# A hybrid decoder layer on one core: its first row tile staged, and the gating, the bank saves and the mix loads of its gated-linear-attention stage put elsewhere

## The chip, the core and the metric

The kernel runs on one core of a Trainium2 chip. TensorE (PE in the rows, PEld for its weight loads) multiplies and transposes into PSUM banks; VectorE (DVE) and ScalarE (ACT) empty the banks; GpSimd (POOL) and SyncE (SP) issue DMAs. Each engine works through its own instructions in order and waits where an operand, a bank or a buffer is not ready. The metric is device microseconds (us) of one execution.

## What is computed

```python
hn = rms_norm(h, norm_mix)
gq, gk, gv, gr, ga, sq, sk, sv = split(hn @ w_in)           # T=1024 rows, D=1024
o_gla = gla_mixer(gq, gk, gv, gr, ga, ...)                  # 4 heads, d_k=64, d_v=128, chunks of 64
o_swa = swa_mixer(sq, sk, sv, rel_bias, sinks)              # window 128
h = h + concat([o_gla, o_swa]) @ w_out
h = h + cross_attn(rms_norm(h, norm_cross), rms_norm(mem, norm_mem), w_q, w_k, w_v, w_o)
h = h + conv_ffn(rms_norm(h, norm_ffn), w_up, conv_w, conv_b, w_down)
return rms_norm(h, norm_final)

# the part of gla_mixer behind the recurrence
o = o * rsqrt(mean(o * o, -1) + EPS) * gla_gain             # per head
return o.reshape(T, 512) * silu(gr)
```

## The kernel before

All data are float32. A product is made of three TensorE passes over operands split into a high and a low part: `split` (L105) has ACT cast the high part (L109, with a gain L112) and DVE subtract it to get the low part (L110, with a gain L113), and `mm3` (L138) multiplies high by high (L140), high by low (L141) and low by high (L142). PSUM has eight banks in this part of the kernel: two with the role F, four S, two O; a tile of a role takes the bank whose last tile has been emptied. Weights pass through three staging buffers (`st`) and six slots (`w`, three pairs), so a load can start only when the split of the load three before it is done.

**The start (`rows_a`, L449).** The 1024 rows of x come in eight row tiles of 128 rows (`load_x`, tiles `gr` and `prob`, 512 KB each); the weights for 272 columns of w_in come in three staged portions, for k = 0 to 2, 3 to 5 and 6 to 7 (`row_weights`, L423). The weights are loaded first, then the row tiles. For each row tile PE transposes eight 128x128 blocks into two S banks (L404), ACT and DVE split them into `xh` and `xl`, ACT sums the squares (`sumsq`, L188), and PE makes 8 x 3 products of 272 columns (`row_tile`). PE's order is written out: it transposes row tiles 0 and 1, then makes the products of tile 0, transposes tile 2, makes the products of tile 1, and so on. DVE multiplies each staged portion by the gain `norm_mix` (L124) ahead of its split. The other engines' order is left to a scheduler.

**The GLA stage (`gla`, L650).** The chunk recurrence runs over four pairs of row tiles (i = 0, 2, 4, 6). For a pair PE makes the state sums (L709) and the attention blocks (L739, two S banks), the outputs (`gla_products`, L758 and L765, two F banks); ACT squares them (L775), DVE sums (L776), both find the reciprocal root, and ACT scales the outputs into `o` (L787, eight instructions). One pair later `gla_output` (L790) transposes `o` into two S banks (L799), DVE gates each bank with `gla_gain` and `gr` (L802, tiles `eb`), and the result is split into `x` tiles (`og`). The orders of PE, DVE and ACT are the program's order here.

Between these steps `more(count)` (L658) runs portions of another job, the cross-attention keys and values of the 256 memory rows. `multiply(n)` makes the products of portion n; `prepare(n + 3)` loads and splits the weights of portion n + 3. Portions 0 to 7 are the values: four of them fill two O banks of 512 columns, which `save` (L346) empties in four pieces of 256 columns (`la`, ACT cast and DVE subtraction in turn, then a store by POOL's queue). Portions 8 to 15 are the keys, one O bank of 256 columns each. The calls are two portions ahead of each pair's products, two more behind the output of the third pair, three behind that of the fourth and four at the end of the loop.

**Behind it.** `swa_mix` (L907) loads the window attention's result from DRAM (`x<-ow_d`, eight loads of 512 KB on SP's queue). `mix_out` (L918) multiplies it and `og` by w_out (loads `st<-in_w_out_dram`, three DMAs a portion), then adds the residual `res`, which SP's queue loads from `xt_d`.

## Time and profile before

| | |
|---|---|
| median of 3 runs | 1338.66 us (1335.7 to 1339.94) |
| profiled execution | 1338.4 us, its span 1336.3 us |
| PE busy in the span | 1306.5 us (98%) |
| DVE, ACT, POOL busy | 920.8, 586.8, 86.4 us |

The profile is one execution; its times run from the start of its span, and 2.1 us of its time lie outside the span. In rows of the timeline the first number is the start, the second the duration, and the square bracket says how long the engine had stood idle before and what ended that.

### The profile page before, as it was taken

The page shows a single profiled execution, that of the slowest core. Times are in us where ns is not written, and L with a number is a line of the kernel's source. Part 1 is how long each engine was busy: PE and PEld are TensorE (multiplying, and loading weights), DVE is VectorE, ACT ScalarE, POOL GpSimd, SP SyncE. Part 2 cuts the span into 40 slices and gives each one's busy share as a digit, 9 for nine tenths or more (in the row PEclk, how much of TensorE's full clock was granted, in tenths as well). Part 3 has the DMA queues.
Part 4 walks back from the last instruction along what each step waited for, and adds up shares of the span by engine and source line. Part 5 has one row for each costly group of instructions (what it writes and reads, how often), then busy time and mean ns, then how long its engine had stood idle before and what let it go on. Part 6 is the DMA issues. An engine that isn't in the chain of part 4 may idle for free.

```text
span 1336.3 us, 17266 instructions
## 1 busy us (share of the span) xinstructions
PE 1306.5 (98%) x6575; PEld 1082.3 (81%) x6575; DVE 920.8 (69%) x1566; ACT 586.8 (44%) x1040; POOL 86.4 (6%) x150
## 2 busy tenths in 40 slices
PE   7999999999899999999999999999999999999997
PEld 6887777988788888888888888888888888788785
DVE  6848763367444344464469998888888887998766
ACT  5425545335333233453334554434443444454454
POOL 1400111101111000001100000000000000000000
PEclk9999999999999999999999999999999999999998
DMA  7642111144954422143321333222232138710203
GB/s 219 178 116 64 60 55 60 63 149 145 294 162 142 134 64 64 31 141 97 95 64 58 115 127 110 95 92 66 79 95 94 65 109 317 267 64 8 72 20 146
DMA packets 141528, 146.89 MB, mean 110 GB/s; under 512 B 15825, under 2 KB 108166, under 8 KB 141446
## 3 DMA queue, kind: packets, MB, share of 16 engines
q1 hardware_dynamic: 129974, 111.02, 27.1%
q0 software_dynamic: 10304, 32.68, 6.9%
q10 hardware_dynamic: 1168, 2.10, 0.4%
q8 instruction: 51, 0.84, 0.3%
q14 instruction: 31, 0.25, 0.1%
HBM read 109.06 MB, written 38.28 MB: 110 GB/s over the span
## 4 chain that ended last, share of the span: by engine, by line
PE 49%; issue 37%; DVE 6%; DMA 4%; POOL 2%; ACT 2%; SPq 1%; POOLq 0%; DVEq 0%; ACTq 0%
PE psF L140 9%; PE psF L142 9%; PE psF L141 9%; PE psF L1262 4%; PE psS L1262 3%; DVE w L110 2%; DMA st<-in_w_out_dram 2%; PE psT L1262 1%; PE psO L1262 1%; PE psO L140 1%; PE psO L141 1%; PE psO L142 1%; PE psO L897 1%; PE psS L844 1%; PE psS L884 1%
## 5 line engine op out<-in xcount | busy, mean ns | idle before, releaser
L109 ACT CAST w<-st 128x1024 fp32r<-128x1024 f32 (+2 forms) x165 | 145.2, 880 | 293.9 <-PE psF L141 106.4
L110 DVE TENSOR_TENSOR w<-st,w 128x1024 fp32r<-128x1024 f32 (+2 forms) x165 | 166.3, 1008 | 91.4 <-ACT w L109 90.4
L1184 DVE SCALAR_TENSOR_TENSOR uy<-uy,vec,uy 128x1023 f32<-128x1023 f32 (+1 forms) x88 | 112.0, 1278 | 0.9 <-ACT uy L1182 0.4
L1262 PE MATMUL psF<-w,w 128*128 128x512 f32 x330 | 92.9, 390 | 0.1
L1262 PE MATMUL psS<-w,w 128*128 128x512 f32 x330 | 92.4, 389 | 0.0
L1155 PE MATMUL psS<-a,w 128*128 128x512 f32 x360 | 86.5, 389 | 0.0
L140 PE MATMUL psF<-xh,w 128*128 128x512 f32 x208 | 82.9, 399 | 0.0
L141 PE MATMUL psF<-xl,w 128*128 128x512 f32 x208 | 81.4, 391 | 0.0
L142 PE MATMUL psF<-xh,w 128*128 128x512 f32 x208 | 81.4, 391 | 0.0
L1155 PEld LDWEIGHTS psS<-a,w 128*128 128x128 f32 x360 | 67.6, 188 | 14.0
L1155 PE MATMUL psF<-a,w 128*128 128x512 f32 x324 | 77.8, 389 | 0.0
L1262 PEld LDWEIGHTS psF<-w,w 128*128 128x128 f32 x330 | 61.8, 188 | 13.8 <-DVE w L110 0.8
L1262 PEld LDWEIGHTS psS<-w,w 128*128 128x128 f32 x330 | 62.0, 188 | 12.9
L1155 PEld LDWEIGHTS psF<-a,w 128*128 128x128 f32 x324 | 60.8, 188 | 12.6
L140 PE MATMUL psF<-act,w 128*128 128x512 f32 x176 | 69.4, 394 | 0.0
L141 PE MATMUL psF<-act,w 128*128 128x512 f32 x176 | 69.1, 392 | 0.0
L142 PE MATMUL psF<-act,w 128*128 128x512 f32 x176 | 68.7, 390 | 0.0
L1182 ACT ACTIVATE uy<-uy,vec 128x1024 f32<-128x1024 f32 x44 | 54.8, 1246 | 24.9 <-DVE uy L1175 17.2
L1155 PE MATMUL psS<-act,w 128*128 128x512 f32 x240 | 57.8, 389 | 0.0
L1155 PE MATMUL psS<-act,wx 128*128 128x512 f32 x240 | 57.6, 389 | 0.0
L1155 PEld LDWEIGHTS psS<-act,w 128*128 128x128 f32 x240 | 45.1, 188 | 9.4
L1155 PEld LDWEIGHTS psS<-act,wx 128*128 128x128 f32 x240 | 45.0, 188 | 9.3
(392 smaller groups left out, 3004.3 us busy)
## 6 DMA issues: line engine op xcount, KB each, us to landing
st<-in_w_up_dram SPq DMA_DIRECT2D x44, 512.0 KB, 3.9
g_d<-uy POOLq DMA_DIRECT2D x22, 512.0 KB, 2.9
act<-in_w_down_dram SPq DMA_DIRECT2D x12, 512.0 KB, 9.7
st<-g_d SPq DMA_DIRECT2D x10, 512.0 KB, 3.9
res<-g_d SPq DMA_DIRECT2D x10, 512.0 KB, 9.2
st<-in_w_in_dram SPq DMA_DIRECT2D x9, 512.0 KB, 6.2
xt_d<-pts POOLq DMA_DIRECT2D x16, 256.0 KB, 4.6
ow_d<-pts POOLq DMA_DIRECT2D x32, 128.0 KB, 3.2
```

Source lines behind the costliest of these rows:

```text
L109: h = nc.scalar.copy(out=hi, in_=src)
L110: l = nc.vector.tensor_tensor(out=lo, in0=src, in1=hi.bitcast(F32), op=ALU.subtract)
L140: mm(out, lhsT=lh, rhs=rh, start=start, stop=False)
L141: mm(out, lhsT=lh, rhs=rl, start=False, stop=False)
L142: mm(out, lhsT=ll, rhs=rh, start=False, stop=stop)
L844: nc.tensor.matmul(ps[u][g][:, t, :nk], lhsT=self.sq[2 * u + t][pr, q], rhs=self.sk[pr, k0:k0 + nk], start=True, stop=True)
L884: nc.tensor.transpose(pp[:, 2 * u + t], probs[u][:, 2 * g + t, j * P:(j + 1) * P], self.ident)
L897: nc.tensor.matmul(po[64 * g:64 * g + 64], lhsT=self.sv[:, k0 // P + j, 64 * g:64 * g + 64], rhs=pts[2 * j + g], start=j == 0, stop=j == n ...
L1155: nc.tensor.matmul(ps, lhsT=b[l][:, q], rhs=a[q][r], start=first and q == 0 and n == 0, stop=first and q == 3 and n == 2, skip_group_check ...
L1182: nc.scalar.activation(out=y, in_=u, func=AF.Identity, scale=self.v("cw2", j), bias=self.v("conv_b", j))
L1184: nc.vector.scalar_tensor_tensor(out=y[:, s:], in0=u[:, :T - s], scalar=self.v(nm, j), in1=y[:, s:], op0=ALU.mult, op1=ALU.add)
L1262: nc.tensor.matmul(ps[i], lhsT=g[:, l, tk], rhs=w[:, r], start=first and k == 0 and m == 0, stop=first and k == n - 1 and m == 2, skip_gro ...
```

## The change

There are four parts.

- `rows_a` is written out for PE, DVE and ACT. Row tile 0 of x is loaded first, row tile 1 behind the second weight portion. The gain is applied in the split, one k at a time (L112 and L113 on 272 columns), so that L124 is gone here. The products of row tile 0 are made in three stages, k = 0 to 2, 3 to 5, 6 to 7, each behind the split of its portion; row tile 1 is transposed ahead of the third stage. The sums of squares and the emptying of the product banks come for two row tiles together.
- `save` empties a value bank in one piece of 512 columns, given back as two steps, the high part and the low part with the stores.
- `more(count, hold=True)` keeps back the steps of its last portion (the save, and the preparation of the portion three later). `gla_output` transposes and gates both banks first, calls `between`, which runs the kept saves, and only then splits; `release` runs the kept preparation, in a loop's pass behind the pair's scaling.
- `swa_mix` becomes a generator; its loads are called behind the outputs of the first and the second pair, two portions each.

```diff
-        def save(src, d, part):
-            t = new("la", [P, 2, MEM], F32R, 4)
-            self.split(src, t[:, 0], t[:, 1])
...
+        def save(src, ds, part):
+            t = new("la", [P, 2, 512], F32R, 2)[:, :, :MEM * len(ds)]
+            def high():
+                nc.scalar.copy(out=t[:, 0], in_=src)
+            def low():
+                nc.vector.tensor_tensor(out=t[:, 1], in0=src, in1=t[:, 0].bitcast(F32), op=ALU.subtract)
+                for q, d in enumerate(ds):
+                    dst = d.rearrange("p (s x m) -> p s x m", s=2, x=2)[:, :, part]
+                    nc.gpsimd.dma_start(out=dst, in_=t[:, :, q * MEM:(q + 1) * MEM].bitcast(F32))
+            return high, low
...
+                (h0, l0), (h1, l1) = (save(banks[i], (v_d[c], v_d[c + 1]), i) for i in range(2))
+                return [h0, h1, l0, l1]
...
+        def split_weights(st, k0, k1):
+            hi, lo = (self.wslot("w", (P, k1 - k0, n)) for _ in range(2))
+            for k in range(k0, k1):
+                hs[k], ls[k] = hi[:, k - k0], lo[:, k - k0]
+                self.split(st[:, k - k0], hs[k], ls[k], self.v("norm_mix", k))
+        xr = [self.load_row(0, keep, new)]
+        st = [load_weights(0, 3), load_weights(3, 6)]
+        xr.append(self.load_row(1, keep, new))
+        st.append(load_weights(6, 8))
+        xr += [self.load_row(i, keep, new) for i in range(2, NT)]
...
+        with self.tc.manual_schedule(engines={e.PE, e.DVE, e.Activation}):
+            transposed(0, 0)
+            split_weights(st[0], 0, 3)
+            transposed(0, 4)
             for i in range(NT):
-                if i < NT - 1:
-                    next(tiles)
-                self.row_tile(i, weights, evac, "FO"[i % 2])
+                ps = self.bank("FO"[i % 2])
+                cuts = (0, 3, 6, NK) if i == 0 else (0, NK)
+                for k0, k1 in zip(cuts, cuts[1:]):
+                    if i == 0 and k0:
+                        split_weights(st[k0 // 3], k0, k1)
+                    if i < NT - 1 and k1 == cuts[-1 if i == 0 else 1]:
+                        transposed(i + 1, 0)
+                        transposed(i + 1, 4)
+                    products(ps, i, range(k0, k1))
+                if i % 2:
+                    for q in (i - 1, i):
+                        factors(q)
+                    evac(i - 1, done)
+                    evac(i, ps)
+                done = ps
...
+            for n in range(count):
+                steps = [*multiply(part), lambda n=part: prepare(n + 3)]
+                part += 1
+                if hold and n == count - 1:
+                    held.extend(steps)
+                else:
+                    for f in steps:
+                        f()
+        def release(count=None):
+            for f in held[:count]:
+                f()
+            del held[:count]
...
-                more(early)
+                more(early, hold=True)
                 if i:
-                    self.gla_output(i - 2, o, new)
-                more(late)
+                    self.gla_output(i - 2, o, new, lambda: release(-1))
+                    next(mixes, None)
+                    next(mixes, None)
+                if late:
+                    release()
+                    more(late, hold=True)
+                release(-1)
                 po = self.gla_products(i, states)
...
                     o = self.gla_scaled(po, r, new)
-            more(16 - part)
-            self.gla_output(NT - 2, o, new)
+                release()
+            more(16 - part, hold=True)
+            self.gla_output(NT - 2, o, new, release)
```

Where the instructions stand before and after is shown at three places. The first is SP's queue at the start of the program, before:

```order
L122 DMA st_101<-in_w_in_dram 128x3x16
L122 DMA st_101<-in_w_in_dram 128x3x128 x2
L122 DMA st_110<-in_w_in_dram 128x3x16
L122 DMA st_110<-in_w_in_dram 128x3x128 x2
L122 DMA st_119<-in_w_in_dram 128x2x16
L122 DMA st_119<-in_w_in_dram 128x2x128 x2
L387 DMA gr_128<-in_x_dram 128x1024
L387 DMA gr_130<-in_x_dram 128x1024
```

and the same place of the change:

```order
L394 DMA gr_101<-in_x_dram 128x1024
L454 DMA st_103<-in_w_in_dram 128x3x16
L454 DMA st_103<-in_w_in_dram 128x3x128 x2
L454 DMA st_107<-in_w_in_dram 128x3x16
L454 DMA st_107<-in_w_in_dram 128x3x128 x2
L394 DMA gr_111<-in_x_dram 128x1024
L454 DMA st_113<-in_w_in_dram 128x2x16
L454 DMA st_113<-in_w_in_dram 128x2x128 x2
L394 DMA gr_117<-in_x_dram 128x1024
```

Row tile 0 (`gr_101`) has moved past all nine weight DMAs, row tile 1 past the third portion's three.

The second place is the GLA stage while the output of the first pair is made. DVE before, from the weights of portion 5 (`w_2848`) to the first split of the output (`psS_2885` and `psS_2895` hold the transposed output, `psO_2699` and `psO_2700` the value banks, `w_2882` the weights of portion 6):

```order
L110 TENSOR_TENSOR w_2848<-st_2845,w_2847 128x1024
L110 TENSOR_TENSOR la_2863<-psO_2699,la_2863 128x256
L110 TENSOR_TENSOR la_2867<-psO_2699,la_2867 128x256
L110 TENSOR_TENSOR la_2871<-psO_2700,la_2871 128x256
L110 TENSOR_TENSOR la_2875<-psO_2700,la_2875 128x256
L110 TENSOR_TENSOR w_2882<-st_2879,w_2881 128x1024
L802 SCALAR_TENSOR_TENSOR eb_2890<-psS_2885,vec,gr_1787 128x256
L802 SCALAR_TENSOR_TENSOR eb_2890<-psS_2885,vec,gr_1944 128x256
L110 TENSOR_TENSOR x_2644<-eb_2890,x_2643 128x2x256
L802 SCALAR_TENSOR_TENSOR eb_2900<-psS_2895,vec,gr_2101 128x256
L802 SCALAR_TENSOR_TENSOR eb_2900<-psS_2895,vec,gr_2202 128x256
L110 TENSOR_TENSOR x_2648<-eb_2900,x_2647 128x2x256
```

DVE in the change, from the weights of portion 4 (`w_2837`) and 5 (`w_2855`) to both splits:

```order
L110 TENSOR_TENSOR w_2837<-st_2834,w_2836 128x1024
L110 TENSOR_TENSOR w_2855<-st_2852,w_2854 128x1024
L866 SCALAR_TENSOR_TENSOR eb_2877<-psS_2872,vec,gr_1794 128x256
L866 SCALAR_TENSOR_TENSOR eb_2877<-psS_2872,vec,gr_1951 128x256
L866 SCALAR_TENSOR_TENSOR eb_2885<-psS_2880,vec,gr_2108 128x256
L866 SCALAR_TENSOR_TENSOR eb_2885<-psS_2880,vec,gr_2209 128x256
L354 TENSOR_TENSOR la_2870<-psO_2706,la_2870 128x512
L354 TENSOR_TENSOR la_2871<-psO_2707,la_2871 128x512
L110 TENSOR_TENSOR x_2651<-eb_2877,x_2650 128x2x256
L110 TENSOR_TENSOR x_2655<-eb_2885,x_2654 128x2x256
```

The gates stand ahead of the saves and of the splits; the weights of portion 6 now stand behind the next pair's scaling and masks. On SP's queue the mix loads stood behind the last key portion; in the change they stand behind the first one (`st_3070`, portion 8), ahead of portion 9 (`st_3088`):

```order
L122 DMA st_3024<-in_w_v_c_dram 128x2x512
L122 DMA st_3070<-in_w_k_c_dram 128x8x128
L981 DMA x_2900<-ow_d 128x1024
L981 DMA x_2901<-ow_d 128x1024
L981 DMA x_2904<-ow_d 128x1024
L981 DMA x_2905<-ow_d 128x1024
L981 DMA x_3062<-ow_d 128x1024
L981 DMA x_3063<-ow_d 128x1024
L981 DMA x_3066<-ow_d 128x1024
L981 DMA x_3067<-ow_d 128x1024
L122 DMA st_3088<-in_w_k_c_dram 128x8x128
L122 DMA st_3212<-in_w_k_c_dram 128x8x128
```

Eight loads of 512 KB have moved past seven weight loads.

The third place is ACT at the end of the GLA stage, behind the last scaling (`o_3447` before, `o_3452` in the change). Before (`psO_3456`, `psO_3485` and `psO_3514` are the banks of portions 13, 14 and 15, `w_3606` and `w_3678` the first two of w_out):

```order
L787 ACTIVATE o_3447<-psF_3403,grs_3435 128x128
L109 CAST la_3481<-psO_3456 128x256
L109 CAST la_3510<-psO_3485 128x256
L109 CAST w_3606<-st_3602 128x1024
L109 CAST la_3539<-psO_3514 128x256
L109 CAST w_3678<-st_3674 128x1024
```

and in the change (`w_3463` holds the weights of portion 15, `w_3601` the first of w_out):

```order
L850 ACTIVATE o_3452<-psF_3408,grs_3440 128x128
L109 CAST w_3463<-st_3461 128x1024
L351 CAST la_3492<-psO_3467 128x256
L351 CAST la_3521<-psO_3496 128x256
L109 CAST w_3601<-st_3597 128x1024
L109 CAST w_3673<-st_3669 128x1024
L351 CAST la_3550<-psO_3525 128x256
```

The weights of portion 15 stood ahead of the last pair's squares before (`w_3398`, not in these rows) and stand behind its scaling now; on PE one product with `w_3601` has also moved ahead of portion 15's.

## Rows read from the trace of the kernel before

**Rows 1.** The page, part 1: busy us, share, instructions.

```profile
PE 1306.5 (98%) x6575; PEld 1082.3 (81%) x6575; DVE 920.8 (69%) x1566; ACT 586.8 (44%) x1040; POOL 86.4 (6%) x150
```

**Rows 2.** Waits of PE, whole span: us in total, times, longest.

```profile
PE psS L404 <- DMA gr<-in_x_dram: 7.5, 1, 7.5
PE psO L140 <- DVE la L110: 2.8, 3, 1.9
...
PE psS L739 <- DVE eb L802: 2.8, 2, 1.7
...
PE psF L140 <- DVE res L960: 1.1, 1, 1.1
PE psF L140 <- ACT w L109: 1.1, 1, 1.1
```

**Rows 3.** Timeline of the start: SP's queue, DVE and PE.

```profile
0.81 4.65 SPq L122 DMA_DIRECT2D st<-in_w_in_dram  x9
...
5.50 2.16 SPq L387 DMA_DIRECT2D gr<-in_x_dram  x4
...
9.22 0.72 DVE L124 TENSOR_TENSOR st<-st,vec 128x544 f32<-128x544 f32 x1
...
10.08 3.67 PE L404 MATMUL psS<-ident,gr 128*128 128x128 f32 x16 [7.46 <-DMA gr<-in_x_dram]
...
18.29 0.37 PE L140 MATMUL psO<-w,xh 128*128 128x272 f32 x1
```

**Rows 4.** One us of the start: busy of each engine, granted clock, DMA share, GB/s.

```profile
9.00:10.00 1.00, 0.00 (x0) 0.00 (x0) 0.94 (x2) 0.00 (x0) 0.00 (x0) 1.00 1.02 372
```

**Rows 5.** Waits of PE between 45 and 275 us.

```profile
PE psS L844 <- DVE mx L853: 0.4, 1, 0.4
```

**Rows 6.** Timeline of the GLA stage, second and third pair: PE.

```profile
287.05 0.50 PE L140 MATMUL psO<-w,wg 128*128 128x512 f32 x1
...
292.74 1.03 PE L799 MATMUL psS<-ident,o 128*128 128x128 f32 x8
...
298.53 0.46 PE L739 MATMUL psS<-gq,gk 64*128 64x128 f32 x2 [1.06 <-DVE eb L802]
```

**Rows 7.** The same timeline: DVE and ACT.

```profile
292.23 1.23 DVE L110 TENSOR_TENSOR w<-st,w 128x1024 fp32r<-128x1024 f32 x1 [0.89 <-ACT w L109]
...
297.51 0.87 DVE L802 SCALAR_TENSOR_TENSOR eb<-psS,vec,gr 128x256 f32<-128x256 f32 x2
...
305.06 2.18 ACT L787 ACTIVATE o<-psF,grs 128x128 f32<-128x128 f32 x8 [1.26 <-DVE grs L182]
...
308.20 1.23 DVE L110 TENSOR_TENSOR w<-st,w 128x1024 fp32r<-128x1024 f32 x1 [0.88 <-ACT w L109]
```

**Rows 8.** Two stretches of the GLA stage, columns as in rows 4.

```profile
300.00:310.00 10.00, 9.31 (x47) 7.72 (x48) 7.74 (x21) 6.17 (x15) 0.00 (x0) 0.83 0.17 56
...
335.00:340.00 5.00, 4.69 (x26) 4.69 (x27) 2.95 (x4) 1.66 (x4) 1.35 (x2) 0.66 1.01 355
```

**Rows 9.** Timeline of the end of the GLA stage: PE and ACT.

```profile
335.31 0.39 PE L140 MATMUL psO<-wg,w 128*128 128x256 f32 x1 [1.93 <-DVE la L110]
...
342.83 1.09 ACT L775 ACTIVATE lse<-psF 128x512 f32<-128x512 f32 x2 [1.53 <-PE psF L765]
...
346.27 2.18 ACT L787 ACTIVATE o<-psF,grs 128x128 f32<-128x128 f32 x8 [0.84 <-DVE grs L182]
348.29 0.75 ACT L109 CAST la<-psO 128x256 fp32r<-128x256 f32 x2
353.17 1.04 ACT L109 CAST w<-st 128x1024 fp32r<-128x1024 f32 x1 [4.13 <-DMA st<-in_w_out_dram]
```

**Rows 10.** DMA issues between 270 and 372 us: KB each, median us to landing.

```profile
st<-in_w_k_c_dram SPq DMA_DIRECT2D x8, 512.0 KB, 3.9
x<-ow_d SPq DMA_DIRECT2D x8, 512.0 KB, 10.3
```

**Rows 11.** One stretch behind the start, columns as in rows 4.

```profile
40.00:60.00 20.00, 20.00 (x110) 16.16 (x110) 18.86 (x40) 6.74 (x13) 11.74 (x25) 1.00 0.85 235
```

More of the change, by code (lines that the diff above doesn't have):

```diff
@@ L460, in evac @@
                 nc.vector.tensor_scalar(out=d[:, i], in0=ps[:, c:c + P], scalar1=r, scalar2=None, op0=ALU.mult)
-        self.xr = []
-        weights = self.row_weights([(1536, 16), (2192, 128), (512, 128)])
-        self.load_x(keep, new, range(NT))
-        tiles = self.prepare_x()
-        with self.tc.manual_schedule(engines={mybir.EngineType.PE}):
-            next(tiles)
-            for i in range(NT):
-                if i < NT - 1:
-                    next(tiles)
-                self.row_tile(i, weights, evac, "FO"[i % 2])
+        cols = ((1536, 16), (2192, 128), (512, 128))
@@ new lines, in rows_a @@
+        xr = [self.load_row(0, keep, new)]
[3 more added lines that the diff above has]
+        xr += [self.load_row(i, keep, new) for i in range(2, NT)]
+        ssq = self.small("ssq", [P, NT], bufs=1)
+        self.rstd = self.const.tile([P, NT], F32, name="rstd_x")
+        self.rstd_bc = self.bc_tile("rbx")
+        xh, xl = (self.xnew("x" + s, (P, NK, T), F32R) for s in "hl")
+        self.x = [(xh[:, k], xl[:, k]) for k in range(NK)]
@@ new lines, in rows_a, with transposed, factors @@
+        self.xact = self.whole(self.x)
+        def transposed(i, k):
+            tk = slice(i * P, (i + 1) * P)
+            ps = self.bank("S").rearrange("p (k t) -> p k t", k=4)
+            for q in range(4):
+                nc.tensor.transpose(ps[:, q], xr[i][:, (k + q) * P:(k + q + 1) * P], self.ident)
+            self.split(ps, xh[:, k:k + 4, tk], xl[:, k:k + 4, tk])
+        def factors(i):
+            self.sumsq(xr[i], ssq[:, i:i + 1], T)
+            if i % 2:
+                self.rsqrt(self.rstd[:, i - 1:i + 1], ssq[:, i - 1:i + 1], D, 2)
@@ L655, in gla, with more @@
         nc = self.nc
-        part = 0
-        def more(count):
+        part, held = 0, []
+        def more(count, hold=False):
             nonlocal part
-            for _ in range(count):
-                multiply(part)
-                prepare(part + 3)
+            for n in range(count):
+                steps = [*multiply(part), lambda n=part: prepare(n + 3)]
                 part += 1
+                if hold and n == count - 1:
[7 more added lines that the diff above has]
+            del held[:count]
         self.og = [[tuple(self.xnew("x", [P, 2, 512], F32R, 16) for _ in range(2)) for _ in range(2)]
@@ L788, in gla_scaled, with gla_output @@
         return o
-    def gla_output(self, i, o, new):
+    def gla_output(self, i, o, new, between):
         nc = self.nc
@@ L794, in gla_output @@
         sl = slice((i % 4) * P, (i % 4 + 2) * P)
+        gated = []
         for u in range(2):
```

66 lines of the change are left out of this document (30 added, 36 removed).

## The prediction

> **What bounds the kernel now.** I read the busy times first: PE has work for 98% of the span [rows 1], so a part of the change is worth what it does to PE's idle time and to its granted clock, and nothing for what it saves elsewhere. Then PE's waits over the whole span [rows 2]. The longest, 7.5 us, is the start, where the transpositions stand until the first row tile of x lands. Four more belong to the GLA stage: 2.8 us behind the emptying of a value or key bank, 2.8 us behind the gates (`eb`), and 1.1 us each behind `res` and a weight of w_out. Third, the waits between 45 and 275 us: 0.4 us [rows 5]. PE therefore hands on what it gains at the start. Last, the granted clock: in 300 to 310 us its mean is 0.83, in 335 to 340 us 0.66 [rows 8], both behind waits [rows 6, 9]. [...]
>
> **The start.** Before, nine weight DMAs stand ahead of the first row tile on SP's queue (0.81 to 5.46 us, the tile's own at 5.50), PE starts at 10.08, its sixteen transpositions take 3.67 us, and the products of row tile 1 begin at 18.29 [rows 3]. From there both programs do the same, so I ask when that point comes now. The bytes are the same: 512 KB at 372 GB/s are 1.4 us [rows 4, 10]; I use 1.3, the stretch being full but for rounding. DVE took up the third weight portion at 9.22 [rows 3]; two row tiles now go ahead of it, so it lands near 9.2 + 2 x 1.3 = 11.8 us. Its two k are split in pieces of 272 columns, which no row has. Nearest: a 256-column cast takes 0.75 / 2 = 0.37 [rows 9], and 544 columns of L124 take 0.72, so 272 take 0.36 [rows 3]. One cast and two subtractions behind it end at 11.8 + 0.37 + 0.72 = 12.9. Three products of 272 columns follow: 24 of 512 take 5.69 us [rows 6], so one of 272 takes 0.126, three 0.4: 13.3. Then eight transpositions, 1.03 at the full clock [rows 6] and 1.84 at that of the start (half of 3.67). Row tile 1's products begin at 14.3 to 15.1; with half a us for the operands' hand-over between engines, 14.8 to 15.6. That is 2.7 to 3.5 us earlier, and I take **2.7**. [...] The upper bound is 3.7.
>
> L124 is gone (three instructions on DVE, off PE's path). The doubled grain of sums and bank emptying lies beside 3.9 us of PE work a row tile (24 x 0.126 + 8 x 0.13 each). Its cover is DVE, which is idle only 1.1 of 20 us in 40 to 60 [rows 11]; should the batching push DVE late there, PE waits up to that 1.1 and more, which I price with the rivals.
>
> [...]
>
> **The gates.** What can be removed in the GLA stage is 2.8 + 2.8 + 1.1 + 1.1 = 7.8 us of waits and at most 3.4 of clock: 11.2. Take the first pair. Its transpositions end with PE's block at 292.74 + 1.03 = 293.8; DVE is then in saves and weights of which one subtraction is 1.23 [rows 7], and the gates of the second bank start at 297.51 and end at 298.4, so PE stands 1.06 us before L739 [rows 6, 7]. With the gates next in line behind the transpositions, and the last weight subtraction (292.23 + 1.23 = 293.5) and one like it ahead of them, four gates at 0.87 a pair end at 294.7 + 1.74 = 296.4, ahead of the 297.5 at which PE asks (298.53 - 1.06). Both waits behind `eb` go, and the clock's 1.7 behind them.
>
> **Bank saves.** Four pieces of 256 columns become two of 512: fewer instructions on ACT and DVE, both idle for part of each portion, so nothing. But the saves now stand behind the gates, and a key or value bank is wanted later by PE. Of the 2.8 us, one wait of 1.93 is at 335.31 [rows 9], the other two are 0.9. I expect the key banks to cost 0.5 still.
>
> **What is held back.** `release` puts the weights of portion 6 behind the second pair's scaling. Before, that scaling ends at 305.06 + 2.18 = 307.24 and DVE's weight follows at 308.20 + 1.23 = 309.43 [rows 7], 2.2 us behind. PE has the next pair's eight transpositions to do in that time (1.03 and the hand-over, 0.2) before it wants the new weights: it waits about **1.0**. At the end the same order costs more. The last squares start at 342.83 and the scaling ends at 346.27 + 2.18 = 348.45, 5.6 us [rows 9]. Behind it ACT now has the weights of portion 15 (1.04), two saves (0.75) and the first weight of w_out (1.04), 2.8 us, and one PE product with that weight has moved ahead of portion 15's. PE has only portions 13 and 14 meanwhile, each 24 products of 256 columns, 5.69 / 2 = 2.85, so 5.7 us. It waits 5.6 + 2.8 - 5.7 = **2.7**, and since PE's clock fell behind a wait of 1.93 there before, I let it fall again (**1.7** not regained). The bound below is no wait and no fall (portion 15's weights split in a gap), that above twice the 2.7.
>
> **The mix loads.** Eight loads of 512 KB go out about 12 portions earlier. Now they land 10.3 us behind their issue, against 3.9 for a key weight [rows 10]. Ahead of w_out they held ACT for 4.13 us until 353.17 [rows 9]; that goes, and with it PE's 1.1 behind `w` and 1.1 behind `res`. In their new place they stand ahead of seven key weights. They are issued from about 295 us on; 4 MB at 372 GB/s take 11.3 us, and DMA was at 0.17 and 56 GB/s in 300 to 310 [rows 8], so the link is free. The first key weight behind them waits for a stage that frees with the split at 308.2 anyway [rows 7]. So I put them at nothing.
>
> [...]
>
> **Sum of the GLA stage:** 11.2 - 1.0 - 2.7 - 1.7 - 0.5 = 5.3 us, with 0 and 8.5 as ends (all four losses doubled gives -0.6; the end's two losses halved and the clock regained gives about 8.5). With the start 8.0. The profiled execution took 1338.4 us (span 1336.3 and 2.1 around it), so 1338.4 - 8.0 = 1330.4; the median of the runs is 0.26 above it. I forecast **1330.5**.
>
> **The rivals.** A change under 0.3%, 4.0 us, is about what a measurement of this kernel can't tell from none.
> - *The end keeps its clock* (chance 0.17). [...]
> - *The start gives nothing* (0.18). The clock stays low through row tile 1's products, or DVE at 18.86 of 20 us [rows 11] can't take the batched sums and makes PE wait later: 1338.6 - 5.3 = 1333.3.
> - *New waits eat half of what GLA gains, or all, and the start's gain with it* (0.10): the held weights and saves are late at each pair, 1 us four times more, and the 1.7 of 300 to 310 is not regained: 8.0 - 4.0 - 1.7 = 2.3, or 1336.3, with 1334 to 1338 around it. The change would then not do what its parts are for.
> - *The other side: the mix loads starve PE* (0.05). Key weights stand behind 4 MB. From the point at which two of them land with a mix load's 10.3 instead of 3.9 us and no split is ahead, PE waits 2 x 6.4 = 12.8 and loses 1.7 of clock: 1338.6 - 8.0 + 12.8 + 1.7 = 1345.1. Against: the slots `w` hold portions ahead.
>
> **How the numbers follow.** Forecast 0.50. The range reaches from the first rival to the upper part of the second and third, 1326.2 to 1336; outside it lie half of the third and the fourth, and the tails of the terms' bounds. Faster by over 0.3% (under 1334.6): the forecast, the first rival, most of the second, less tails, 0.78. Within: 0.16. Slower: 0.06.
>
> **What would show it.** Right: the first transpositions at 4 to 5 us (issued at 0.81, and a load of its size takes 3.9 [rows 3, 10]); row tile 1's products near 15; no wait of the attention blocks (L739, L802 in the change) on the gates; ACT's 4.13 us and the `res` wait gone; a wait of about 1 us at the first product behind the second pair's transpositions; one of about 2.7 at the first product with w_out, the clock under 0.8 there. Wrong: row tile 1's products past 17 us with the clock low; PE waiting in 45 to 275 for `rstd` or a bank of S; a PE wait on `w` behind a key load; DVE's gates starting over 2 us behind their transpositions.

## The result and the profile after

The change takes 1331.26 us (median of 5 runs, 1329.49 to 1331.29) against 1337.87 before (5 runs): ratio 0.9948, 95% interval 0.9933 to 0.9962, or 6.6 us. The profiled execution spans 1329.2 us, 7.1 less than before. The page's busy times hardly move against [rows 1]:

```profile
PE 1307.0 (98%) x6575; PEld 1083.6 (82%) x6575; DVE 918.0 (69%) x1564; ACT 587.6 (44%) x1041; POOL 86.6 (7%) x150
```

What moved is what PE waits for. (In this fence and in those below rows are picked from a view; the rows between them are left out.) PE's waits over the whole span, where [rows 2] had 7.5 us at the first transpositions, 2.8 behind the banks, 2.8 behind the gates and 1.1 each for `res` and a weight:

```profile
PE psF L140 <- ACT w L109: 2.4, 1, 2.4
PE psO L140 <- DVE la L354: 2.0, 1, 2.0
PE psS L484 <- DMA gr<-in_x_dram: 1.5, 1, 1.5
...
PE psO L141 <- DVE w L110: 0.7, 1, 0.7
```

The gates and `res` have left the list, and two waits of 2 us and more stand in it that [rows 2] doesn't have. The start, the timeline of PE and of ACT:

```profile
4.71 1.97 PE L484 MATMUL psS<-ident,gr 128*128 128x128 f32 x8 [1.54 <-DMA gr<-in_x_dram]
7.11 0.60 PE L140 MATMUL psF<-w,xh 128*128 128x272 f32 x1 [0.42 <-ACT w L112]
...
11.66 1.71 PE L484 MATMUL psS<-ident,gr 128*128 128x128 f32 x8
...
14.75 0.37 PE L140 MATMUL psO<-w,xh 128*128 128x272 f32 x1
...
11.20 0.93 ACT L112 ACTIVATE w<-st,vec 128x272 fp32r<-128x272 f32 x2 [1.60 <-DMA st<-in_w_in_dram]
```

Row tile 0 is transposed at 4.71, its first products run at 7.11, and those of row tile 1 begin at 14.75 instead of 18.29 [rows 3]. The third weight portion is cast at 11.20, before PE has done the first two. The GLA stage, the timelines of DVE, PE, ACT and SP's queue:

```profile
291.21 1.66 DVE L866 SCALAR_TENSOR_TENSOR eb<-psS,vec,gr 128x256 f32<-128x256 f32 x4
291.80 5.91 SPq L981 DMA_DIRECT2D x<-ow_d  x8
294.10 1.16 PE L802 MATMUL psS<-gq,gk 64*128 64x128 f32 x16
302.83 0.50 PE L141 MATMUL psO<-w,wg 128*128 128x512 f32 x1 [0.66 <-DVE w L110]
302.80 26.80 SPq L122 DMA_DIRECT2D st<-in_w_k_c_dram  x7
312.29 1.04 ACT L109 CAST w<-st 128x1024 fp32r<-128x1024 f32 x1 [5.20 <-PE psS L772]
313.24 1.07 ACT L351 CAST la<-psO 128x512 fp32r<-128x512 f32 x2
315.25 0.38 PE L140 MATMUL psO<-wg,w 128*128 128x256 f32 x1 [2.01 <-DVE la L354]
339.16 2.18 ACT L850 ACTIVATE o<-psF,grs 128x128 f32<-128x128 f32 x8 [0.85 <-DVE grs L182]
341.18 1.09 ACT L109 CAST w<-st 128x1024 fp32r<-128x1024 f32 x1
342.11 0.71 ACT L351 CAST la<-psO 128x256 fp32r<-128x256 f32 x2
342.64 2.07 ACT L109 CAST w<-st 128x1024 fp32r<-128x1024 f32 x2
343.82 0.56 PE L140 MATMUL psF<-x,w 128*128 128x512 f32 x1 [2.43 <-ACT w L109]
```

The attention blocks (294.10) follow without the two waits of [rows 6, 7]. At 302.83 PE waits 0.66 us for the weights of portion 6, at 343.82 it waits 2.43 for w_out. And at 315.25 it waits 2.01 us ahead of the first key portion: the save of the value banks (313.24) stands on ACT behind a cast at 312.29, which ACT idled 5.20 us for. That cast is of portion 9's weights, whose load was issued at 302.80, right behind the mix loads: 9.5 us from issue to cast, where a key load took 3.9 us before [rows 10]. Behind both waits PE's granted clock is below 1 (windows; columns as in [rows 4]):

```profile
316.00:331.00 15.00, 14.89 (x112) 14.51 (x112) 13.55 (x30) 8.44 (x19) 4.39 (x7) 0.89 0.67 216
343.00:349.00 6.00, 5.18 (x30) 5.12 (x31) 3.46 (x5) 1.71 (x2) 1.39 (x2) 0.72 0.70 210
```

The DMA engines, which were busy for 0.17 of 300 to 310 us before [rows 8], are full there now (share and GB/s are the last two columns):

```profile
300.00:310.00 10.00, 9.34 (x53) 7.75 (x51) 7.11 (x11) 4.66 (x8) 0.67 (x1) 1.00 1.04 404
```

The first state sums and the last transpositions of `o`, two rows of before and then two of the change:

```profile
274.34 0.32 PE L709 MATMUL psS<-gva,ke 64*64 64x128 f32 x1
...
352.17 1.04 PE L799 MATMUL psS<-ident,o 128*128 128x128 f32 x8
271.04 0.32 PE L772 MATMUL psS<-gva,ke 64*64 64x128 f32 x1
...
348.52 1.04 PE L863 MATMUL psS<-ident,o 128*128 128x128 f32 x8
```

So the total came out near the forecast, 1331.26 against 1330.5. The lead of the changed execution over the one before, one execution of each, says how: it is 3.5 us at row tile 1's products (18.29 - 14.75), 3.3 at GLA's first state sums (274.34 against 271.04), 3.65 behind GLA's last transpositions (353.21 against 349.56), and 7.1 at the end. The stage itself gained only 0.35 us, with one product of w_out taken into it 0.6. Behind it 2.15 us are the two waits for w_out and `res`, which are gone, and the other 1.1, apart from that product's 0.24, stand in code that is the same in both.

### The profile page after: what moved, and what is told of

The parts are those of the page before. It is cut to its first block, busy times and chain, and to the rows that moved or that the text cites. A ratio compares the mean times of both kernels' runs of the same rounds, so it can differ in the third digit from the quotient of the medians.

```text
span 1329.2 us, 17255 instructions
## 1 busy us (share of the span) xinstructions
PE 1307.0 (98%) x6575; PEld 1083.6 (82%) x6575; DVE 918.0 (69%) x1564; ACT 587.6 (44%) x1041; POOL 86.6 (7%) x150
## 4 chain that ended last, share of the span: by engine, by line
PE 50%; issue 37%; DVE 6%; DMA 3%; POOL 2%; ACT 1%; SPq 0%; POOLq 0%; DVEq 0%; ACTq 0%
PE psF L140 10%; PE psF L141 10%; PE psF L142 10%; PE psF L1331 4%; PE psS L1331 3%; DVE w L110 2%; PE psT L1331 1%; PE psO L1331 1%; PE psO L140 1%; PE psO L141 1%; PE psO L142 1%; PE psO L964 1%; PE psS L911 1%; PE psS L951 1%; POOL g_d L1264 1%
## 5 line engine op out<-in xcount | busy, mean ns | idle before, releaser
L109 ACT CAST w<-st 128x1024 fp32r<-128x1024 f32 (+1 forms) x162 | 142.5, 883 | 282.9 <-PE psF L141 110.0
L110 DVE TENSOR_TENSOR w<-st,w 128x1024 fp32r<-128x1024 f32 (+1 forms) x162 | 163.6, 1012 | 86.4 <-ACT w L109 85.8
```

The costliest lines, as they stand in the source:

```text
L109: h = nc.scalar.copy(out=hi, in_=src)
L110: l = nc.vector.tensor_tensor(out=lo, in0=src, in1=hi.bitcast(F32), op=ALU.subtract)
```

## Experiments

All times have a run of the kernel before beside them; its medians were 1337.5 to 1338.5 us. The *stage* below runs from the start of the first state sums to the end of the last transpositions of `o`; of the trace before it is 353.21 - 274.34 = 78.87 us, of the change 78.5, or 78.3 without the product of w_out in it. Stages and waits are those of one execution each. The run without the stages of the start, below, has the change's GLA stage unaltered, and its stage is 77.4 us against 78.5: a difference of about 1 us between two stages shows nothing. The intervals of the times are 1.7 to 2.2 us to either side.

**The new start alone.** `load_row` and `rows_a` of the change in the kernel before, nothing else.

```diff
-        self.xr = []
-        weights = self.row_weights([(1536, 16), (2192, 128), (512, 128)])
-        self.load_x(keep, new, range(NT))
...
+        xr = [self.load_row(0, keep, new)]
+        st = [load_weights(0, 3), load_weights(3, 6)]
+        xr.append(self.load_row(1, keep, new))
...
```

> The kernel before with the new start alone (row tile 0 ahead, gain in the split, products of row tile 0 in three stages). First theory: the start is worth its own share and PE hands it on. Row tile 1's products begin at 14.7 to 14.8 us instead of 18.29, the lead at GLA's first state sums is 3.3 us, and the time falls by about 3.3 us (ratio 0.9975), with the waits behind the gates (2.8 us) and the banks (2.8 us) still there. Rival: a later stage waits for something that doesn't come sooner (DMA, the gates), and gives most of the lead back: less than 1.5 us are left at the end.

Measured: 1332.34 us, ratio 0.9962 (0.9948 to 0.9976), 5.1 us below before. The waits in the stage are as before:

```profile
13.65 0.37 PE L140 MATMUL psO<-w,xh 128*128 128x272 f32 x1
294.13 0.46 PE L777 MATMUL psS<-gq,gk 64*128 64x128 f32 x2 [1.05 <-DVE eb L840]
296.29 1.21 PE L777 MATMUL psS<-gq,gk 64*128 64x128 f32 x14 [1.71 <-DVE eb L840]
330.75 0.39 PE L140 MATMUL psO<-wg,w 128*128 128x256 f32 x1 [1.94 <-DVE la L110]
```

The first theory holds: row tile 1's products begin at 13.65 and the lead at the state sums is 4.4 us. That is more than was expected, but it is the earliest of eleven executions with this start (13.65 to 15.44), and the expected 3.3 us lie inside the time's interval (3.2 to 7.0 us). The start is most of the change's gain; all that it does in the GLA stage adds about 1 us (1332.34 to 1331.26), less than these intervals resolve.

**The start without its stages.**

```diff
+                if i == 0:
+                    split_weights(st[1], 3, 6)
+                    transposed(1, 0)
+                    transposed(1, 4)
...
-                    if i < NT - 1 and k1 == cuts[-1 if i == 0 else 1]:
+                    if 0 < i < NT - 1:
```

> The change with the first products not staged: row tile 0 still comes first, but PE transposes row tile 1 ahead of all products of row tile 0 (and the second weight portion is split ahead of it). First theory: what staging buys is that PE works off its first products, at the lower of its two rates, while it would otherwise wait for row tile 1. Then PE waits for row tile 1 until about 9.5 us, its rate rises 1.5 to 2.5 us later than in the change, and row tile 1's products begin at 16 to 17.5 us instead of 14.75 (13.65 to 15.4 in the runs with staging so far); the time rises by 1.5 to 2.5 us. Rival: the start is bound by the landing of the third weight portion, and the order of PE ahead of it is worth nothing: row tile 1's products begin by 15.4 us and the time is that of the change.

Measured: 1332.74 us, ratio 0.9962 (0.9947 to 0.9977); the trace:

```profile
4.72 1.97 PE L484 MATMUL psS<-ident,gr 128*128 128x128 f32 x8 [1.48 <-DMA gr<-in_x_dram]
10.17 1.97 PE L484 MATMUL psS<-ident,gr 128*128 128x128 f32 x8 [3.48 <-DMA gr<-in_x_dram]
16.88 0.37 PE L140 MATMUL psO<-w,xh 128*128 128x272 f32 x1
```

PE waits 3.48 us for row tile 1, and row tile 1's products begin at 16.88, 2.1 us later than in the change, and the time is 1.5 us above the change's: the first theory. The row tile ahead of the weights, with the rest of the rewritten start, is worth 1.4 us (18.29 to 16.88), the stages the rest.

**Saves in 512 columns, in their old place,** with the new start and the change's `save`.

```diff
-            for _ in range(count):
-                multiply(part)
-                prepare(part + 3)
+            for _ in range(count):
+                for f in multiply(part):
+                    f()
+                prepare(part + 3)
```

> The new start, and of the GLA stage's parts only the saves in 512 columns, in their old place ahead of the gates. First theory: nothing but a fraction of a us: four subtractions of 0.42 us become two of 0.64, so that DVE comes to the gates 0.4 us sooner, and the two waits behind the gates (1.05 and 1.71 us) shrink by up to 0.4 each: the stage is 78 to 78.7 us and the time within 1 us of the new start alone. Rival: the larger saves free the banks later or earlier by enough to change the waits ahead of the key portions by 1 us or more.

Measured: 1331.08 us, ratio 0.9951 (0.9938 to 0.9965), within 1.3 us of the new start alone. In the trace the first wait behind the gates is gone, and of the second, 1.71 us in the new start alone, 1.00 are left. The banks cost PE 2.06 and 2.31 us where the new start alone has 1.94 and 0.60; this shift of the waits is the rival's.

```profile
294.90 1.13 PE L786 MATMUL psS<-gq,gk 64*128 64x128 f32 x14 [1.00 <-DVE eb L849]
343.19 0.39 PE L140 MATMUL psO<-wg,w 128*128 128x256 f32 x1 [2.31 <-DVE la L354]
293.00:303.00 10.00, 9.00 (x70) 7.32 (x63) 8.03 (x22) 5.99 (x16) 0.67 (x1) 1.00 0.45 140
```

The granted clock behind the gates holds (1.00 in 293 to 303 us; with the new start alone the same window has 0.83). The stage is 76.8 us against 78.7 with the new start alone, so that 1.9 us of the stage come with the larger saves alone, the gates in their old place. In time no difference is shown.

**The mix loads back behind the stage,** the rest of the change kept.

```diff
-                    next(mixes, None)
-                    next(mixes, None)
...
                     self.gla(new, prepare, multiply)
+                    list(self.swa_mix())
```

> The change with the mix loads called behind the GLA stage again, as before it. First theory: the 2.0 us that PE waits ahead of the first key portion, and the low clock behind it, come from the eight mix loads: the weights of portion 9 land behind them, and the saves of the value banks stand behind that portion's cast on ACT. Then that wait falls to under 0.5 us and the granted clock of the 15 us behind it is 1.00, which is worth 3.5 us; at the end of the stage w_out stands behind the mix loads again and PE waits 1 to 2 us for a weight or the residual. In all about 1329.5 us, 1.5 to 2.5 below the change. Rival: the saves are late because they are held behind the gates and come in 512 columns; then the 2.0 us stay, and the time is that of the change or 1 to 2 us above it.

Measured: 1328.82 us, ratio 0.9938 (0.9925 to 0.9950). The wait ahead of the first key portion is gone, and the clock behind it holds: the two key portions take 5.94 us (313.91 to 319.85) where the change takes 7.46 (315.25 to 322.71). So the 2.01 us come from the mix loads, as the first theory has it. But little of it is kept in the stage: PE waits 0.92 us ahead of portion 13, and

```profile
342.94 0.58 PE L140 MATMUL psO<-wg,w 128*128 128x256 f32 x1 [3.55 <-DVE la L354]
```

ahead of portion 15; the stage is 77.6 us (271.79 to 349.36).

**The saves ahead of portion 9's weights,** the mix loads early. The step `prepare(9)` goes behind the saves of the value banks.

```diff
                 if hold and n == count - 1:
-                    held.extend(steps)
+                    held[:] = [*steps[:-1], *held, steps[-1]]
+                elif behind:
+                    held.append(steps[-1])
...
-                    more(late, hold=True)
+                    more(late, hold=True, behind=i == 4)
```

> The change with one thing moved: in the third pair the saves of the two value banks stand ahead of the split of portion 9's weights on ACT and DVE, and the mix loads stay early. First theory (portion 9's weights are late behind the mix loads, and the saves queue behind their cast): the wait of 2.0 us ahead of the first key portion falls to 0.3 us or less, the clock behind it stays at its upper level, and the time falls by about 3.5 us to 1327.8. The weights of portion 9 are late as before (ACT's 5.2 us of idle time stay), but PE wants them only a portion later. Rival: the mix loads' traffic or the held saves delay the banks themselves: 1 us or more of the wait stays and the time is within 1.5 us of the change.

Measured: 1329.68 us, ratio 0.9941 (0.9928 to 0.9953). The first key portion starts without a wait (312.80), so the queue on ACT is what made it wait. But ACT's squares of the third pair stand behind the late cast as well, and the scaling is late instead:

```profile
319.57 1.10 PE L865 MATMUL psS<-ident,o 128*128 128x128 f32 x7 [0.52 <-ACT o L852]
322.87 0.58 PE L140 MATMUL psO<-wg,w 128*128 128x256 f32 x1 [2.19 <-DVE la L354]
```

The wait has moved by two portions. The mechanism is right, but of its price of 3.5 us 1.6 are won.

**The end of the stage.** Portion 15's weights ahead of the last squares; w_out's first splits behind the saves of portions 13 and 14, PE's first product with it behind portion 15.

```diff
-                release(-1)
+                release(None if i + 2 == NT else -1)
                 po = self.gla_products(i, states)
...
+            with self.tc.issue_after(self.la14[0]), self.tc.issue_after(self.la14[1]):
+                w2 = self.load(pieces)
+            with self.tc.issue_after(self.last.ins):
+                self.proj_t(w2, lambda k, h: self.mix[k, h], evac, order=(4, 5, 6, 7, 0, 1, 2, 3))
```

> The change with the end of the stage put in another order: the weights of portion 15 are split ahead of the last pair's squares (as before the change), the first two splits of w_out stand behind the saves of portions 13 and 14, and PE's first product with w_out behind portion 15. First theory: what PE waits 2.4 us for is ACT's and DVE's queue behind the last scaling (two weight splits ahead of or around the save of portion 13), not the scaling itself. The wait falls to 0.8 us or less, portion 15 runs at the upper clock (2.9 us instead of 4.5), and the time falls by about 3.3 us to 1328. Rival: the scaling itself ends too late for the 5.7 us of products that PE has; then 2 us or more of waiting stay ahead of portion 15 and the time is within 1 us of the change.

Measured: 1328.77 us, ratio 0.9939 (0.9926 to 0.9951). PE waits 1.51 us ahead of portion 15 (0.8 or less was expected), and portion 15 takes 3.10 us instead of 4.51: the wait is 0.9 us shorter than the change's 2.43, and the 1.4 us of clock are back. The queue behind the scaling is thus shown as 0.9 us of the wait; 1.5 are left, more than the first theory allows and less than the rival. Nor does the clock prove the new order, for with the change's own order and a wait of 2.29 us portion 15 kept its clock as well (last section). In this execution the first key portion waits 3.11 us and the two key portions take 8.64, so that the stage is 77.5 us. The idle time of ACT ahead of portion 9's cast has its true releaser here:

```profile
312.82 1.04 ACT L109 CAST w<-st 128x1024 fp32r<-128x1024 f32 x1 [6.32 <-DMA st<-in_w_k_c_dram]
```

**The gates alone:** the new start, gates behind the transpositions with the saves behind them, mix loads behind the stage, no preparation held.

```diff
-                release(-1)
+                release()
                 po = self.gla_products(i, states)
```

(and the mix loads back as above)

> The new start, the gates behind the transpositions with the saves behind the gates, and nothing else of the change in the GLA stage: mix loads behind the stage, no preparation held back. First theory: the gates' order alone is worth the two waits behind the gates and the slower products that follow them (2.8 and 1.5 us), against the new start alone. The stage is then 74.5 us against 78.7 with the new start alone; at its end stand 1 to 2 us of waits for w_out, as with the new start alone. The time is 1328 to 1329. Rival: PE, which comes earlier, waits for banks and scalings instead, so the stage is 77 us or more and the time within 2 us of the new start alone.

Measured: 1326.01 us, ratio 0.9910 (0.9895 to 0.9925), and a stage of 73.7 us (271.09 to 344.82) against 78.7 with the new start alone (269.95 to 348.66). The first theory's mechanism holds: the gates, with the saves in 512 columns behind them, are worth 5.0 us of the stage, of which 1.9 had come with the saves alone, so that 3.1 are left for the order of the gates. The time is 2 us or more below the one expected, and the waits for w_out that it expected at the end are not there. Against the run with the mix loads back this one differs only in the preparations, and its stage is 3.8 us shorter: that is what holding them costs there (2.8 in time). Its one wait in the stage is left ahead of portion 15:

```profile
339.30 0.39 PE L140 MATMUL psO<-wg,w 128*128 128x256 f32 x1 [2.98 <-DVE la L354]
```

**No preparation held, mix loads early.** The fourth case of the two parts.

> The change with no preparation of weights held back, the eight mix loads still together behind portion 8's weights. With it the four cases of the two parts are there (stage from first state sums to last transpositions: held and early 78.3 us, held and behind the stage 77.6, not held and behind 73.7). First theory: both parts cost by themselves; holding costs 0.7 us at portion 6, and the mix loads cost the 2.0 us ahead of the first key portion with 1.5 us of lower clock behind it. Then the wait at portion 6 is gone, that ahead of the first key portion stays at 2 to 3 us, the stage is 75.5 to 77.5 us, the time 1328 to 1330. Rival: the mix loads only cost because the held preparation pushes the saves back; then the wait ahead of the first key portion is under 0.7 us, the stage 74 us and the time 1326.

Measured: 1325.23 us, ratio 0.9904 (0.9890 to 0.9917). ACT still idles for portion 9's load, and PE still waits ahead of the first key portion:

```profile
311.15 1.05 ACT L109 CAST w<-st 128x1024 fp32r<-128x1024 f32 x1 [4.99 <-DMA st<-in_w_k_c_dram]
...
314.11 0.39 PE L140 MATMUL psO<-wg,w 128*128 128x256 f32 x1 [1.60 <-DVE la L354]
```

The two key portions behind it keep the upper clock here (5.94 us). The stage is 75.3 us (271.25 to 346.54) with five products of w_out in it, about 74.1 without. Not holding the preparations takes 4.2 us off the stage of the change and 6.0 off its time. That PE waits at the first key portion is the first theory's, the time is below what either gave. Against their place behind the stage, the early mix loads cost 0.4 us of the stage here (73.7) and 0.7 with the preparations held (77.6), less than two executions of one code differ by; in time this run is 0.8 us faster than the gates alone, the change 2.4 slower than with the loads back. Behind the stage they stand ahead of w_out and of the last key weights. What a better place is worth the run with single mix loads shows.

**A third buffer for the key portions' saves,** on the run with the gates alone.

```diff
+            if len(ds) == 1 and self.saves % 3 == 2:
+                t = new("lk", [P, 2, MEM], F32R, 1)
+            else:
+                t = new("la", [P, 2, 512], F32R, 2)[:, :, :MEM * len(ds)]
```

> The run with the gates' order alone, and a third buffer for the key portions' saves (every third one goes to a buffer of its own; the change has two buffers of 512 columns where the kernel before has four of 256). First theory: in that run the saves of portions 11 and 12 waited for the stores of the saves two before (ACT idle 4.8 and 1.55 us behind a store), which put a weight cast ahead of the last squares and the squares 1.8 us behind PE's products; with the third buffer the squares start within 0.6 us of them, the wait ahead of portion 15 falls from 3.0 to 1.5 us or less, portion 15 keeps the upper clock, and the time falls by 1.5 to 2.5 us to about 1324. Rival: the squares wait for the weight cast anyway (its load lands late), and nothing changes.

Measured: 1325.14 us, ratio 0.9906 (0.9892 to 0.9919). The squares now start 0.1 us behind PE's products (329.94, in the run with the gates alone 332.26 and 1.8 behind), the wait ahead of portion 15 falls from 2.98 to 1.20 us, portion 15 keeps the upper clock (3.1 us instead of 4.3), and the stage is 70.4 us instead of 73.7. Of this 3.3 us little is left in the time: PE then waits for w_out, whose load stands behind the mix loads. The first of these rows is of the run with the gates alone:

```profile
328.17 0.37 ACT L351 CAST la<-psO 128x256 fp32r<-128x256 f32 x1 [4.80 <-DMA k_d<-la]
...
336.94 0.39 PE L140 MATMUL psO<-wg,w 128*128 128x256 f32 x1 [1.20 <-DVE lk L359]
342.48 0.50 PE L140 MATMUL psF<-x,w 128*128 128x512 f32 x1 [1.56 <-ACT w L109]
```

In time that is inconclusive (1326.01 to 1325.14), but it shows that the two buffers made the saves wait for their stores, and that this cost the stage 3.3 us.

**Mix loads one by one, and the end's order.**

```diff
             elif n < 16:
                 weights[n] = self.load_cols(a["w_k_c"][0], (n - 8) * P)
+            if n in range(4, 12):
+                next(self.mixes)
```

(with each load put behind the last DMA of SP's queue by `issue_after`)

> The change with the end of the stage ordered as in the run of that name, and the mix loads one by one: 512 KB behind the load of each of the portions 4 to 11, instead of eight together behind portion 8's. First theory: no key weight is then late by more than one to three mix loads, so the wait ahead of the first key portion (2.0 us in the change, 3.1 with the end's order) falls to 0.7 us or less, the clock behind it stays up, and the GLA stage from its first state sums to its last transpositions shrinks from 78.3 us to about 74; the time is about 1326. Rival: the length of the stage is set by the chain of ACT and DVE from pair to pair, and a wait that is taken away comes back behind it, as it did in part when the saves went first: the stage stays at 77 us or more, the time at 1328.5 to 1330.

Measured: 1325.07 us, ratio 0.9904 (0.9887 to 0.9920), stage 72.5 us (270.31 to 342.79). The first key portion doesn't wait; 0.66 us at portion 6, 0.55 and 1.20 ahead of later key portions are left. The first theory holds, with 1.5 us more than it asked for. Not all loads went out singly: two did ahead of 274 us, three together behind portion 8's weights at 291.05, the last three singly behind those of portions 9 to 11. Portion 9's load takes 5.3 us from issue to cast (9.5 in the change):

```profile
302.07 0.38 SPq L122 DMA_DIRECT2D st<-in_w_k_c_dram  x1
...
307.35 1.05 ACT L109 CAST w<-st 128x1024 fp32r<-128x1024 f32 x1 [1.00 <-DMA st<-in_w_k_c_dram]
```

The DMA engines are about as full as in the change (share 0.90 in 300 to 310 us, 1.04 there), which speaks for the load's place in the queue and against the full link as the cause. The loads' spacing is all that sets this run apart from that with the end's order: 5.0 us of the stage (77.5 to 72.5), 3.7 of the time.

**The same, nothing held back.** The edit of the gates alone on top.

> The run before this one, with no preparation of weights held back: each pair's last portion of weights is split ahead of that pair's squares, as before the change, and only the saves are held, for the gates. First theory: holding the preparation costs PE 0.7 us at portion 6 and puts a weight split ahead of a save behind each later scaling. Then the 0.65 us at portion 6 go, the wait ahead of portion 15 is under 1 us, and the stage is 1 to 2 us shorter than in the run before: about 73 us, a time of about 1325. Rival: the split ahead of the squares delays the scaling by its 1.05 us at each pair; the transpositions or the banks wait for it instead, and the time is that of the run before or more.

Measured: 1323.48 us, ratio 0.9891 (0.9876 to 0.9905), the fastest: 14.6 us below before and 7.8 below the change. The first theory holds, with 2.4 us of the stage where it asked for 1 to 2. The stage is 70.1 us (271.58 to 341.68), with one wait, and the granted clock in 300 to 340 us is 1.00:

```profile
337.70 0.39 PE L140 MATMUL psO<-wg,w 128*128 128x256 f32 x1 [0.75 <-DVE la L354]
```

```profile
300.00:340.00 40.00, 39.25 (x378) 36.84 (x377) 30.45 (x58) 24.78 (x53) 8.20 (x12) 1.00 0.81 250
```

## Why the prediction was right, and where it was not

The time, its sign and the range were right. The split was not: of 8.0 us the prediction gave 2.7 to the start and 5.3 to the GLA stage; the trace gives the start 3.5 and the stage with the waits behind it 0.6 + 2.15 = 2.75, and 1.1 us lie where nothing was changed and stay without a cause. Two errors went against each other, and that they nearly cancelled is luck. No run shows the 1.7 us that the sum takes for each stretch of lower clock; the runs show 1.55 us behind the gates (24 products of 512 columns from 301.75 to 309.00 us before, from 295.19 to 300.89 in the change), 1.5 at the two key portions (7.46 against 5.94) and 1.4 at portion 15 (4.51 against 3.1).

**The start (2.7 taken, upper bound 3.7).** The mechanism was right, its size too low, and one step of the chain was wrong. The prediction let the third weight portion's landing (11.8) set the end of row tile 0's products (13.3). It was cast at 11.20 in the trace, while PE was still at work on the first two portions: from 7.64 us PE waits for nothing. What goes with the time is when PE's rate rises: at 10.5 us with the new start alone, whose products of row tile 1 begin at 13.65, at 14.4 without the stages, where they begin at 16.88. In eleven executions with this start, row tile 1's products began between 13.65 and 15.44 us, a lead of 2.9 to 4.6 us. The rival that gave the start a worth of nothing had the clock stay low through row tile 1's products; in the change these are 0.125 us apart, the upper rate. The products of the first two stages do run at the lower rate (0.226 us apart), but this is work done in time that PE would have waited (3.48 us for row tile 1 in the run without stages), and its rate rises earlier than there (11.7 to 13.1 us in the change, 14.4 without the stages). That rival is out, and so is its other half, the batched sums: between 45 and 275 us PE waits 0.4 us, as before [rows 5]. One sum was off without consequence: 24 x 0.126 + 8 x 0.13 is 4.1 us a row tile, not 3.9; the trace has 3.9 (14.75 to 18.64).

**The gates (2.8 and 1.7 us removed).** Right in mechanism: both waits are gone in the change, and the gates with the 512-column saves are worth 5.0 us of the stage by themselves (4.5 forecast). But 1.9 of the 5.0 belong to the saves, which the prediction put at nothing. The gates at 297.51, which it took for the second bank's, are the first bank's; the second's follow behind the first split, with the wait of 1.71. Its four gates end ahead of PE either way.

**The held preparations.** Right in mechanism and size: 0.66 us at portion 6 (1.0 forecast); at the end 2.43 us (2.7), and portion 15 at 4.51 us instead of 3.1 (1.7 forecast for the clock). That is 4.5 us of 5.4. The clock's part is no constant: with the same order and a wait of 2.29 us portion 15 kept its clock in the run without stages (3.0 us). Which wait comes last there differs from the prediction's single chain: by DVE's rows the portion's bank, behind two splits and a save on ACT and DVE, came free no earlier than PE began the w_out product, so it would have held PE about as long; no run separates the two. The pairs of runs with and without held preparations give 3.8 and 4.2 us of the stage, 2.8 and 6.0 of the time.

**The mix loads ("I put them at nothing").** This step failed. The prediction let the key weight behind them wait for a staging buffer and no longer, and called the link free by the DMA share of 0.17 before. The key weight did wait for a buffer, and went out at 302.80 when one came free; but with 4 MB issued ahead of it on the queue since 291.80, and the share at 1.04, it took 9.5 us more until the cast. (The loads moved past seven weight loads, not 12 portions.) The wait of 2.01 us that followed, and 1.5 us of lower clock (7.46 us for two key portions instead of 5.94), are the fourth rival's mechanism with one late load in place of two. In the run with spaced mix loads, with DMA about as full (share 0.90 in 300 to 310 us against 1.04), the 9.5 us are 5.3 and PE doesn't wait at the first key portion. The rival's slots `w`, which were to cover a late weight, did; what they didn't cover is the save that stood behind the late cast on ACT. What the block costs depends on the rest: put behind the stage, or with the saves ahead of the cast, no more than 0.7 to 1.1 us come off the stage, as the next wait of the same chain (scaling, weight split, save) takes its place; with the end in order, single loads take off 5.0.

**Bank saves ("so nothing", 0.5 for the banks).** In time nothing clear of the noise, but neither term was right. By themselves the larger saves take 1.9 us off the stage. And overlooked: with four buffers of 256 columns turned into two of 512, a key portion's save waits for the store of the one two before it; with the gates alone that put the last squares 1.8 us behind PE's products and cost 3.3 us of the stage (0.9 of the time, inside the noise).

**The waits for w_out and `res`.** Right: the waits for w_out's load and for `res` are gone in the change. The 2.43 us at w_out's first product are another, for its split.

## What to carry to other kernels

On an engine with a written order, put a split that may wait for a load behind the save that PE needs, and look at what else stands behind that split. Put a load that nothing needs soon between urgent ones, not ahead of them in a block. Count the buffers when a tile grows: two large ones in place of four cost 3.3 us of the stage here, as the third buffer showed. When a wait is removed from a chain that runs from engine to engine, look for the next instruction in the same queue before counting the gain: each repair of the mix loads or of the end alone won 1.6 to 2.5 us, the release of the preparations 6.0, and all together 7.8. And a total that fits is no evidence for its terms: the lead along the trace and the run of the start alone showed that the stage had gained almost nothing.

## What the runs showed of the hardware

The granted clock in the windows doesn't show PE's slow start. In the change its column reads 1.00 in 9 to 10 us, where products of 272 columns are 0.226 us apart, and 1.00 in 14 to 15 us, where they are 0.125 apart:

```profile
9.00:10.00 1.00, 1.00 (x6) 1.00 (x6) 1.00 (x4) 0.60 (x2) 0.00 (x0) 1.00 1.19 282
14.00:15.00 1.00, 1.00 (x11) 1.00 (x10) 0.72 (x2) 0.40 (x1) 0.00 (x0) 1.00 1.00 401
```

272 columns are 1.2 a ns at the first spacing and 2.2 at the second. The moment of the rise differs between executions of the same start: 10.5 us with the new start alone, between 11.7 and 13.1 us in the change, though PE worked without a pause from about 7.6 us in both. What sets it stays open.

Nor does the length of a wait tell whether the clock falls behind it. Behind 1.93 us it fell before (0.66 in 335 to 340 us [rows 8]), behind 2.01 and 2.43 us in the change. In the run without stages PE waited 2.29 us where the change waits 2.43, and portion 15 behind it ran in 3.0 us, not 4.51; with the saves in 512 columns it waited 2.31 us, and portion 15 took 3.1.

```profile
346.38 0.50 PE L140 MATMUL psF<-x,w 128*128 128x512 f32 x1 [2.29 <-ACT w L109]
346.00:350.00 4.00, 3.62 (x30) 3.57 (x31) 3.03 (x5) 1.28 (x2) 1.39 (x2) 1.00 0.66 192
```

A releaser can be wrong: ACT's 5.20 us ahead of portion 9's cast stand in the change's trace as a wait for PE, and as one for the DMA in other runs with the same order there, among them the run without stages, whose GLA stage is the change's (5.75 us). The cast reads `st`, not the bank that the row names.
